# One layer of a hybrid decoder on one core: 12 of 16 n-tiles of the per-layer gate as seven block products

## The chip, the cores and the metric

The kernel runs on one core of a Trainium2 chip. The metric is the device time of one execution in microseconds, from the first instruction to the last; the time before is the median of 3 runs. Engines are named as in the profile: PE (matrix products; PEld its weight loads), DVE (vector), ACT (scalar and table functions), POOL (GpSimd), SP (which only issues DMAs). Each engine works through its own instructions in order; ACT and POOL issue DMAs too.

## What is computed

One layer over 512 prompt tokens and 8 sample tokens, all in float32, D = 2048. Left out here are the norms of queries and keys, the masks and the caches that are handed back:

```python
xn = rmsnorm(x)
q, k, v, gu, gv = split(xn @ w_in)
a = window_attention(q, k, v) @ w_br_attn
m = (gelu(gu) * (W_s @ layernorm(gelu(gv)) + b)) @ w_br_gm          # the gating unit
gB, gA = split(sigmoid(xn @ w_gate + b_gate))
x = x + (gA * a + gB * m) @ w_out
h = causal_conv3(rmsnorm(x) @ w_up)
x = x + (silu(h_gate) * h_up) @ w_down                              # 5632 wide
y = x + sigmoid(rmsnorm(x) @ w_ple_gate) * (p @ w_ple_proj)         # the per-layer gate
```

## The kernel before

**Layout.** Activations lie transposed: a tile holds 128 features by 520 tokens, in two halves of 260 (HW) with 256 prompt and 4 sample tokens each. Tiles of this size live in 67 slots of SBUF (`slot`, NSLOT); some names go to a small extra pool instead (`extra`). A product is taken as three: every float32 operand is split into a rounded part hi and a remainder lo, and hi*hi + hi*lo + lo*hi is summed in PSUM.

**Weights.** They come in blocks of 8 tiles of 128 x 128 (512 KB). `weight_stream` fixes their order for the whole kernel. `block_start(v)` runs as the first tile of block v is used: it issues the loads that are due (SP, three blocks ahead for a plain block), casts block v+2 to hi on ACT, takes its remainder lo on DVE (`cast_block`, `rest_block`), and runs what was put off to this block with `at_block(ahead, f, kind)`, in the order snap, act, dve, end. hi and lo have three buffers each, so ACT casts block v+2 once PE has left block v-1. The order of the instructions is written out by hand; nothing is rescheduled.

**Plain n-tiles.** `ntile` computes one output tile of 128 features from nk input tiles: per weight tile 2 halves x 3 products = 6 matmuls of 260 columns. After each weight tile it advances the generator `self.fine` by one call, so that other work is spread between the tiles.

**Seven block products.** `wpair` computes two n-tiles at once over pairs of k-tiles. Of the 2 x 2 blocks (two n-tiles, two k-tiles, two halves of the tokens) it forms seven products (Strassen's scheme in Winograd's form) in the order P1, P5, P6, P2, P4, P7, P3, each one a block of up to 8 weight tiles with 3 matmuls a tile. The weight sums are made by DVE additions and by POOL DMAs that add while they load (L310, L312). P1, P2 and P3 take halves of the input as they are, the other four take sums of halves; `woperands` builds those and splits them into tiles X. Four PSUM banks collect the outputs; `snap`, `c11`, `c22` and `c12` (L403 to L419) read them.

**Stages.** The front (w_in, attention); `branch_attn` (a = attn @ w_br_attn) with `gmlp`, the gating unit, as its `self.fine`; `gates_plain`, 6 plain n-tiles of w_gate while the operands X are built from x read back from DRAM; `gates_seven`, the other 26 n-tiles; `branch_gm`; `w_out` with p @ w_ple_proj, whose output goes to DRAM (`ppd`); `ffn_up`, all by seven products; `ffn_down`, the k-tiles of w_down in chunks FF_CHUNKS = (6, 14, 6, 12, 6), plain and seven products in turn, where each plain chunk also builds the operands of the next and each chunk but the last adds its output to `x1d` in DRAM; `down_last`, the last chunk, where x stays in SBUF in 16 slots (`self.x1`) and is split into xw; `ple`, the gate by w_ple_gate, 16 plain n-tiles, the last in two halves.

**The gating unit.** `gmlp` is a generator of steps. Each of four chunks of tokens takes two: transposes on PE with statistics on DVE, then the normalisation on DVE (L1298). Each of eight d takes three: the scaling by nw with the split (L1310 to L1312), nothing, then the mix on PE (L1320, L1321) with its sums on DVE. Then come the statistics of the sample tokens (L1332 to L1345), nothing, and their product gx (L1351). `paced` in `branch_attn` leaves 3 weight tiles between two steps.

**Building operands.** `build` takes one operand a call (or `group` of them): `begin` forms the sum on DVE and issues the ACT cast at once, `end` takes the remainder on DVE one call later.

Of the kernel before, what the change touches and what calls it, by code (L numbers as in the profile page):

```python
# [37 lines left out]
PLAIN_GATES = 6  # L38
OUT_GROUP = 3
# [9 lines left out]
FF_CHUNKS = (6, 14, 6, 12, 6)  # L49
# [94 lines left out]
def weight_stream():  # L144
# [26 lines left out]
    for n in range(KD):  # L171
        o.nt("pgate", n, range(KD))
    return o.done()
# [23 lines left out]
class Kernel:  # L197
# [196 lines left out]

    def wpair(self, name, n1, n2, X):

# [24 lines left out]
        after = {"P5": [("snap", lambda: snap("b", "sn", 1))], "P1": [("snap", lambda: snap("a", "sn", 0))], "P2": [("dve", c11)],  # L421
                 "P6": [("snap", lambda: snap("a", "un", 0))], "P7": [("snap", lambda: snap("a", "un", 1)), ("dve", c22)],
                 "P3": [("dve", c12)]}
        for p in PRODUCTS:
# [11 lines left out]
            for kind, f in after.get(p, ()):  # L436
                self.at_block(0, f, kind)
        return c

    def woperands(self, xb):  # L440
# [4 lines left out]
        def begin(p, i):  # L445
# [3 lines left out]
            if p == "P5":  # L449
                src = self.slot(name="tau")[:, 0:HW]  # L450
                nc.vector.tensor_sub(src, b11, b12)
            elif p == "P6":
                nc.vector.tensor_sub(b12, b22, b12)
                nc.vector.scalar_tensor_tensor(out=b11, in0=b12, scalar=-1.0, in1=b11, op0=ALU.mult, op1=ALU.subtract)
                src = b11
            elif p == "P4":
                nc.vector.tensor_add(b21, b21, b11)
                src = b21
            else:
                src = {"P1": b11, "P2": b21, "P7": b12, "P3": b22}[p]  # L460
            x = self.slot(F32R, "X")
            nc.scalar.copy(x[:, 0:HW], src)

            def end():
                nc.vector.tensor_sub(x[:, HW:NT], src, x[:, 0:HW].bitcast(F32))
                X[p][i] = x

            return end
# [95 lines left out]
    def run(self):  # L564
# [62 lines left out]
        with ExitStack() as c2:  # L627
# [11 lines left out]
            self.ffn_down(c3)  # L639
            c3.close()  # L640
            self.slotp = {}
        with ExitStack() as c1:
            self.psum(c1, 2, 4)
            self.down_last()
            self.ple()
# [84 lines left out]
    def branch_attn(self):  # L730
# [48 lines left out]
    def gates_plain(self):  # L779

        nc, a, xn = self.nc, self.a, self.xn
        X = {p: [None] * KQ for p in PRODUCTS}
# [3 lines left out]
        xb = {}  # L786
        self.X, build = self.woperands(xb)
        self.X.update(X)

        def run():  # L790
            for i in range(KQ):
                for k in (2 * i, 2 * i + 1):
                    xb[k] = self.slot(name="xr")
                    nc.sync.dma_start(xb[k][:, 0:NT], a["x"][k])
                yield
                yield
                yield
                yield
                for k in (2 * i, 2 * i + 1):
                    nc.scalar.activation(xb[k][:, 0:NT], xb[k][:, 0:NT], AF.Copy, scale=self.col("an", k))  # L800
# [3 lines left out]
        self.fine = run()  # L804
# [444 lines left out]
    def gmlp(self):  # L1249
# [58 lines left out]
        for d in range(KG):  # L1308
# [3 lines left out]
            h, l = self.split(self.v2(gv[d]), "gn")  # L1312
            yield
            yield
# [16 lines left out]
            yield  # L1331
# [15 lines left out]
        yield  # L1347
# [433 lines left out]
```

## Time and profile before

| | us |
|---|---|
| median of 3 runs (2702.42 to 2703.47) | 2703.02 |
| profiled execution | 2702.04 |
| its span | 2700.3 |

The profiled execution's time is 1.7 us more than its span, from the first to the last instruction of the program. The page gives the busy time of each engine, then the span in 40 slices, the DMA queues, the chain of work that ended last, and the costliest groups. Of the stages, with bounds read from the order of PE's instructions: the front runs to 393 us, w_br_attn and the gating unit to 515, the plain gates to 585, the seven-product gates to 846, w_br_gm to 938, w_out to 1122, p @ w_ple_proj to 1150, the up-projection to 2039, the five chunks of w_down to 2108, 2250, 2319, 2441 and 2511, and the per-layer gate to 2696.

How to read the rows that follow: a row of waits names the waiting group, what it waited for, us in total, times, and the longest. A row of stages gives the stretch, its length, the busy us of PE, PEld, DVE, ACT and POOL (instructions in brackets), the granted clock of PE, the DMA share and GB/s. A row in order of time gives start, us, engine, line, what, count, and in square brackets the idle time before it and what ended it. A row of groups gives the count, busy us, mean ns, and the idle time before.

### The profile page before, as it was taken

What the parts mean: (1) busy time and instruction counts of PE and PEld (TensorE: products, weight loads), DVE (VectorE), ACT (ScalarE), POOL (GpSimd) and SP (SyncE); (2) the same over time, 40 slices, a digit from 0 to 9 for tenths busy, and PEclk for the clock granted to TensorE, in tenths of its full rate; (3) what the DMA queues carried; (4) which work ended last, traced back from release to release, by engine and by line L of the source; (5) the groups of instructions that cost most, each with busy time, mean ns of one, the idle gap of its engine ahead of it and who ended that gap; (6) DMA issues with size and microseconds to landing.
All of it is one profiled execution on the core that took longest, in us unless ns stands there. A gap on an engine that the chain in (4) does not pass through costs nothing.

```text
span 2700.3 us, 53713 instructions
## 1 busy us (share of the span) xinstructions
PE 2673.4 (99%) x22212; PEld 2668.0 (99%) x22212; DVE 1871.6 (69%) x2791; ACT 1287.4 (48%) x2173; POOL 288.4 (11%) x443
## 2 busy tenths in 40 slices
PE   9999999999999999999999999999999999999999
PEld 9999998999999999999999999999999999999999
DVE  6666557567666533688888888888888676576533
ACT  5365452354444233555555555555556445444321
POOL 0111001000010000011111111111111111110000
PEclk9999999999999999999999999999999999999999
DMA  5223323567667444566666666666668677675333
GB/s 188 93 81 102 103 79 122 184 206 204 190 188 239 158 134 142 193 186 171 163 177 174 162 174 174 162 177 171 166 167 249 152 180 204 153 178 183 125 132 106
DMA packets 151797, 438.06 MB, mean 162 GB/s; under 512 B 17200, under 2 KB 18352, under 8 KB 151552
## 3 DMA queue, kind: packets, MB, share of 16 engines
q1 hardware_dynamic: 117504, 337.58, 37.1%
q0 software_dynamic: 29440, 88.53, 18.8%
q10 hardware_dynamic: 4608, 8.52, 0.8%
q8 instruction: 174, 2.85, 0.4%
q14 instruction: 71, 0.58, 0.1%
HBM read 373.23 MB, written 61.33 MB: 161 GB/s over the span
## 4 chain that ended last, share of the span: by engine, by line
PE 96%; DVE 2%; ACT 1%; issue 0%; DMA 0%; POOL 0%; ACTq 0%; SPq 0%; DVEq 0%; POOLq 0%
PE wa L433 22%; PE wb L433 15%; PE mm L372 14%; PE mm L376 14%; PE mm L374 14%; PE wd L433 7%; PE wc L433 7%; PE po L1106 1%; PE s L1043 1%; ACT hi L279 0%; PE pt L1088 0%; PE pl L1654 0%; DVE lo L286 0%; DVE z L1298 0%; ACT z L1256 0%
## 5 line engine op out<-in xcount | busy, mean ns | idle before, releaser
L286 DVE TENSOR_TENSOR lo<-st,hi 128x1024 fp32r<-128x1024 f32 (+3 forms) x352 | 421.9, 1198 | 268.9 <-ACT hi L279 261.3
L433 PE MATMUL wa<-X,hi 128*128 128x260 f32 x3152 | 576.6, 283 | 0.9 <-ACT pp L1427 0.9
L433 PEld LDWEIGHTS wa<-X,hi 128*128 128x128 f32 x3152 | 485.5, 188 | 1.1 <-ACT pp L1427 1.1
L279 ACT CAST hi<-st 128x1024 fp32r<-128x1024 f32 (+3 forms) x352 | 362.3, 1029 | 195.8 <-DMA st<-in_w 83.8
L433 PE MATMUL wa<-X,lo 128*128 128x260 f32 x1576 | 444.7, 282 | 0.0
L433 PE MATMUL wb<-X,hi 128*128 128x260 f32 x2032 | 371.5, 283 | 0.0
L279 ACT CAST hi<-S 128x1024 fp32r<-128x1024 f32 (+2 forms) x219 | 222.6, 1017 | 230.0 <-DVE S L312 171.7
L286 DVE TENSOR_TENSOR lo<-S,hi 128x1024 fp32r<-128x1024 f32 (+2 forms) x219 | 258.5, 1180 | 99.9 <-ACT hi L279 99.6
L433 PEld LDWEIGHTS wb<-X,hi 128*128 128x128 f32 x2032 | 312.8, 188 | 0.0
L433 PEld LDWEIGHTS wa<-X,lo 128*128 128x128 f32 x1576 | 296.7, 188 | 0.0
L433 PE MATMUL wb<-X,lo 128*128 128x260 f32 x1016 | 286.7, 282 | 0.0
L286 DVE TENSOR_TENSOR lo<-L,hi 128x1024 fp32r<-128x1024 f32 (+2 forms) x146 | 172.5, 1181 | 125.0 <-ACT hi L279 124.6
L372 PE MATMUL mm<-xn,hi 128*128 128x260 f32 x1088 | 222.9, 286 | 5.3 <-ACT hi L279 5.3
L376 PE MATMUL mm<-xn,lo 128*128 128x260 f32 x1088 | 219.6, 283 | 0.0
L374 PE MATMUL mm<-xn,hi 128*128 128x260 f32 x1088 | 219.3, 283 | 0.0
L279 ACT CAST hi<-L 128x1024 fp32r<-128x1024 f32 (+2 forms) x146 | 148.4, 1016 | 121.3 <-PE wd L433 118.8
L433 PE MATMUL wd<-X,hi 128*128 128x260 f32 x1120 | 205.1, 283 | 0.0
L310 POOL DMA_DIRECT2D L<-in_w x73 | 63.3, 867 | 1265.5 <-issue 828.9
L433 PEld LDWEIGHTS wb<-X,lo 128*128 128x128 f32 x1016 | 191.4, 188 | 0.0
L372 PEld LDWEIGHTS mm<-xn,hi 128*128 128x128 f32 x1088 | 168.4, 190 | 5.4 <-ACT hi L279 5.3
L433 PEld LDWEIGHTS wd<-X,hi 128*128 128x128 f32 x1120 | 172.2, 188 | 0.1
L376 PEld LDWEIGHTS mm<-xn,lo 128*128 128x128 f32 x1088 | 168.8, 189 | 0.0
(313 smaller groups left out, 5966.8 us busy)
## 6 DMA issues: line engine op xcount, KB each, us to landing
st<-in_w SPq DMA_DIRECT2D x317, 512.0 KB, 4.4
S<-in_w SPq DMA_DIRECT2D x57, 512.0 KB, 3.5
S<-in_w POOLq DMA_DIRECT2D x57, 512.0 KB, 7.9
L<-in_w SPq DMA_DIRECT2D x57, 512.0 KB, 4.0
L<-in_w POOLq DMA_DIRECT2D x57, 512.0 KB, 5.6
fd<-hb SPq DMA_DIRECT2D x44, 260.0 KB, 2.2
fr<-fd SPq DMA_DIRECT2D x44, 260.0 KB, 4.9
xr<-in_x SPq DMA_DIRECT2D x32, 260.0 KB, 4.2
```

The lines of the kernel that those rows point to most:

```text
L279: self.nc.scalar.copy(self.hi[v][:, c], self.st[WS.src[v]][:, c])
L286: self.nc.vector.tensor_sub(self.lo[v][:, c], self.st[WS.src[v]][:, c], self.hi[v][:, c].bitcast(F32))
L310: self.nc.gpsimd.dma_start(self.st[kind, r][:, c], self.a["w"][src][:, c], accum_op=ALU.add)
L372: mm(ps[:, h, 0:HW], lhsT=whi, rhs=xh[h], start=start, stop=False)
L374: mm(ps[:, h, 0:HW], lhsT=whi, rhs=xl[h], start=False, stop=False)
L376: mm(ps[:, h, 0:HW], lhsT=wlo, rhs=xh[h], start=False, stop=stop)
L433: nc.tensor.matmul(ps(z), lhsT=w, rhs=x, start=new and i == 0 and q == 0, stop=i == len(X[p]) - 1 and q == 2, skip_group_check=True)
L1043: nc.tensor.matmul(out, lhsT=self.cols(q, c), rhs=keys(kk, c), start=n == 0, stop=n == 1)
L1106: nc.tensor.matmul(po[:, kb * 128:kb * 128 + w], lhsT=vv[:, kb * 128:(kb + 1) * 128], rhs=pp[:, o:o + w], start=kb == 0 and n == 0, stop=k ...
```

## The change

1. The per-layer gate: `ple` becomes `ple_plain`, 4 plain n-tiles (PLAIN_PLE), and `ple_seven`, 12 n-tiles in 6 pairs. Before, x1 stayed in SBUF; now `down_last` also writes it to `x1d` and splits it into two halves a tile, `ple_plain` reads it back to build the operands (`sum_operands`, which is `gates_plain`'s builder made general), and each output tile reads p @ w_ple_proj and x1 again (`y_load`). The last pair finishes by hooks in `wpair`.
2. The gating unit: steps 4 weight tiles apart; the split for d+1 is issued a step ahead of the mix of d, and the sample statistics ahead of all mixes.
3. Operands in three steps: sum, cast, remainder, each one call later than the one before.
4. FF_CHUNKS = (5, 14, 5, 14, 6), and the builder there takes two calls for every fourth step only, in place of every second.
5. `c21`, the last part of the second output, is formed as P3 begins, not after it.

```diff
+PLAIN_PLE = 4
-FF_CHUNKS = (6, 14, 6, 12, 6)
+FF_CHUNKS = (5, 14, 5, 14, 6)
...
-    for n in range(KD):
+    for n in range(PLAIN_PLE):
         o.nt("pgate", n, range(KD))
+    for n in range(PLAIN_PLE, KD, 2):
+        o.winograd("pgate", n, n + 1, range(KD))
...
+        def c21():
+            nc.vector.tensor_sub(part("c2", 0), ps("d"), part("un", 1))
+
         def c12():
             nc.vector.tensor_add(part("c1", 1), ps("b"), part("un", 0))
-            nc.vector.tensor_sub(part("c2", 0), ps("d"), part("un", 1))
...
         def build(items, every=1, group=1):
-            ends = []
-            while items or ends:
+            hi, lo = [], []
+            while items or hi or lo:
                 for _ in range(every if isinstance(every, int) else next(every)):
                     yield
-                now, items = items[:group], items[group:]
-                new = [begin(*x) for x in now]
-                for e in ends:
-                    e()
-                ends = new
+                for f in lo:
+                    f()
+                for f, _ in hi:
+                    f()
+                lo = [f for _, f in hi]
+                new = [steps(*x) for x in items[:group]]
+                items = items[group:]
+                for f, _, _ in new:
+                    f()
+                hi = [f[1:] for f in new]
...
         def paced():
             for _ in g3:
-                yield
-                yield
-                yield
+                yield from [None] * 4
...
+    def sum_operands(self, xn, src, w):
...
         def run():
             for i in range(KQ):
                 for k in (2 * i, 2 * i + 1):
                     xb[k] = self.slot(name="xr")
-                    nc.sync.dma_start(xb[k][:, 0:NT], a["x"][k])
...
+                    nc.sync.dma_start(xb[k][:, 0:NT], src[k])
+                yield from [None] * 3
                 for k in (2 * i, 2 * i + 1):
-                    nc.scalar.activation(xb[k][:, 0:NT], xb[k][:, 0:NT], AF.Copy, scale=self.col("an", k))
+                    nc.scalar.activation(xb[k][:, 0:NT], xb[k][:, 0:NT], AF.Copy, scale=self.col(w, k))
                 yield from build([(p, i) for p in ("P5", "P6", "P4", "P7")], 1)
...
+        hl = parts(0)
+        yield
         g = [self.slot(name="gn") for _ in range(2)]
         ag, rs = stats(banks, NS)
...
         yield
-        yield
+        for d in range(KG):
+            new = parts(d + 1) if d + 1 < KG else None
+            yield
+            mix(d, *hl)
+            hl = new
+            yield
         p = self.aux("gx")
...
-                    X, self.fine = self.down_operands(ch[c + 1], cycle((1, 2)))
+                    X, self.fine = self.down_operands(ch[c + 1], cycle((1, 1, 1, 2)))
...
+        def parts(n):
+            self.xw[n] = self.split_halves(x1[n], "yw", self.col("pn", n))
+            t = x1.pop(n)
+            self.at_block(1, lambda: nc.sync.dma_start(self.x1d[n], t[:, 0:NT]))
...
+    def ple_plain(self):
+        nc = self.nc
+        self.X, self.fine = self.sum_operands(self.xw, self.x1d, "pn")
+        yl = self.y_load(0)
+        for n in range(PLAIN_PLE):
+            p = self.ntile("pgate", n, range(KD), self.xw)
+            self.drain(self.gr)
+            t = self.slot(name="pg")
+            nc.vector.tensor_mul(self.v2(t), self.pv(p), self.v2(self.R))
+            fs = self.y_end(n, lambda t=t: t, yl)
+            self.at_block(0, fs[1], "act")
+            self.at_block(1, fs[2], "dve")
+            self.at_block(1, fs[3])
+            if n + 1 < PLAIN_PLE:
+                yl = self.y_load(n + 1)
+        self.finish_fine()
+        self.xw = None
+
+    def ple_seven(self):
+        h0, h1 = slice(0, HW), slice(HW, NT)
+        for n in range(PLAIN_PLE, KD - 2, 2):
+            c = self.wpair("pgate", n, n + 1, self.X)
+            for i in range(2):
+                self.y_blocks(i + 1, self.y_end(n + i, lambda c=c, i=i: c[f"c{i + 1}"], self.y_load(n + i)))
...
+        def first(c):
+            y.extend((self.y_load(n), self.y_load(n + 1)))
+            self.y_blocks(0, self.y_end(n, lambda: c["c1"], y[0], h0))
+
+        def second(c):
+            for f in self.y_end(n + 1, lambda: c["c2"], y[1]):
+                self.at_block(0, f)
+
+        c = self.wpair("pgate", n, n + 1, self.X, {"P4": first, "P7": second})
+        self.flush()
+        for f in self.y_end(n, lambda: c["c1"], y[0], h1):
+            f()
```

`y_load` issues two loads on SP (p @ w_ple_proj and x1 of tile n) into the extra pool's four buffers; `y_end` returns four steps for an output tile: times R on DVE, sigmoid on ACT, times p and plus x1 on DVE, the store on SP; `y_blocks` puts them off by up to two blocks.

More of the change, by code (lines that the diff above doesn't have):

```diff
@@ L443, in woperands, with steps, own, hi @@
         X = {}
-        def begin(p, i):
+        def steps(p, i):
             k1, k2 = xb[2 * i], xb[2 * i + 1]
             b11, b12, b21, b22 = k1[:, 0:HW], k1[:, HW:NT], k2[:, 0:HW], k2[:, HW:NT]
[L449 to L464, printed above, removed]
+            src = {"P1": b11, "P2": b21, "P6": b11, "P4": b21, "P7": b12, "P3": b22}.get(p)
+            x = None
+            def own():
+                nonlocal src
+                if p == "P5":
+                    src = self.slot(name="tau")[:, 0:HW]
+                    nc.vector.tensor_sub(src, b11, b12)
+                elif p == "P6":
+                    nc.vector.tensor_sub(b12, b22, b12)
+                    nc.vector.scalar_tensor_tensor(out=b11, in0=b12, scalar=-1.0, in1=b11, op0=ALU.mult, op1=ALU.subtract)
+                elif p == "P4":
+                    nc.vector.tensor_add(b21, b21, b11)
+            def hi():
+                nonlocal x
+                x = self.slot(F32R, "X")
+                nc.scalar.copy(x[:, 0:HW], src)
+            def lo():
@@ L1306, in bc, with parts @@
             return z.rearrange("p (h c w) -> p h c w", h=1, c=1).to_broadcast([128, 2, 2, 128])
-        for d in range(KG):
+        def parts(d):
             w = nw[d // 4][:, (d % 4) * 128:(d % 4) * 128 + 128]
@@ L1311, in gmlp, with mix @@
             nc.gpsimd.dma_start(a["gp_o"][:, d * 128:(d + 1) * 128], self.cols(gv[d], 3))
[L1312 to L1314 removed]
+            return self.split(self.v2(gv[d]), "gn")
+        def mix(d, h, l):
             ps = [self.aux("mx") for _ in range(2)]
@@ L1614, in down_last @@
             del self.f[j]
-        self.finish_fine()
-        xw[KD - 1] = self.split(self.v2(self.x1[KD - 1]), "yw", scale=self.col("pn", KD - 1))
-        self.xw = xw
+        parts(KD - 1)
         self.R = self.slot(name="R3")
@@ L1620, in down_last, with y_load @@
         self.bg.append(self.gr)
-    def ple(self):
-        nc, a = self.nc, self.a
-        pp = {}
-        def load(n):
-            if n < KD:
-                pp[n] = self.slot(name="pp")
-                nc.sync.dma_start(pp[n][:, 0:NT], self.ppd[n])
-        load(0)
-        load(1)
-        for n in range(KD - 1):
-            load(n + 2)
+    def y_load(self, n):
+        t = [self.slot(name="yl") for _ in range(2)]
+        self.nc.sync.dma_start(t[0][:, 0:NT], self.ppd[n])
+        self.nc.sync.dma_start(t[1][:, 0:NT], self.x1d[n])
+        return t
@@ new lines, in y_end, with times_r, sigmoid, rest @@
+    def y_end(self, n, t, yl, c=slice(0, NT)):
+        nc = self.nc
+        pp, x1 = yl
+        def times_r():
+            nc.vector.tensor_mul(t()[:, c], t()[:, c], self.R[:, c])
+        def sigmoid():
+            nc.scalar.activation(t()[:, c], t()[:, c], AF.Sigmoid)
+        def rest():
+            nc.vector.tensor_mul(t()[:, c], t()[:, c], pp[:, c])
+            nc.vector.tensor_add(t()[:, c], t()[:, c], x1[:, c])
+        def store():
+            nc.sync.dma_start(self.a["y_o"][n][:, c], t()[:, c])
+        return times_r, sigmoid, rest, store
@@ L1636, in ple, with y_blocks @@
+    def y_blocks(self, b, fs):
+        for i, (f, kind) in enumerate(zip(fs, ("dve", "act", "dve", "end"))):
+            self.at_block(b + min(i, 2), f, kind)
+    def ple_plain(self):
+        nc = self.nc
+        self.X, self.fine = self.sum_operands(self.xw, self.x1d, "pn")
+        yl = self.y_load(0)
+        for n in range(PLAIN_PLE):
             p = self.ntile("pgate", n, range(KD), self.xw)
             self.drain(self.gr)
-            g = self.slot(name="pg")
-            nc.vector.tensor_mul(self.v2(g), self.pv(p), self.v2(self.R))
```

74 lines of the change are left out of this document (27 added, 47 removed).

## The prediction

> **What bounds the kernel now.** I read the page first, its busy times and the chain that ended last.
>
> ```profile
> span 2700.3 us, 53713 instructions
> PE 2673.4 (99%) x22212; PEld 2668.0 (99%) x22212; DVE 1871.6 (69%) x2791; ACT 1287.4 (48%) x2173; POOL 288.4 (11%) x443
> PE 96%; DVE 2%; ACT 1%; issue 0%; DMA 0%; POOL 0%; ACTq 0%; SPq 0%; DVEq 0%; POOLq 0%
> ```
>
> TensorE (PE) is busy all but 26.9 us of the span and holds 96% of the chain. So time changes in two ways only: by the number of matmuls, or by the stalls and slow clock of PE. The chain in order of time gives the price of a matmul, and the list of waits, for PE alone, gives the stalls.
>
> ```profile
> 585.08 2.88 PE wa L433 x24
> ```
>
> ```profile
> PE mm L372 <- ACT hi L279: 5.3, 1, 5.3
> PE mx L1320 <- ACT gnh L490: 3.7, 1, 3.7
> PE mm L372 <- ACT pp L1427: 2.6, 3, 1.4
> PE gx L1351 <- DVE dgs L1344: 2.2, 1, 2.2
> PE g L1294 <- DVE z L1298: 2.0, 3, 0.8
> ...
> PE mx L1321 <- DVE gnl L491: 0.6, 2, 0.4
> ```
>
> A block of 24 matmuls of 260 columns takes 2.88 us, 0.120 us each; a plain weight tile (6 matmuls) takes 0.72 us and a block of eight of them 5.77 us. Of the stalls, the rows mx, gx, g and mx, 8.5 us, are all of the gating unit, which runs in steps beside the product of w_br_attn. The table of stages shows that two of them cost more than the wait, since the granted clock (PEclk) falls afterwards:
>
> ```profile
> 425.00:429.10 4.10, 0.38 (x5) 0.18 (x3) 3.27 (x10) 0.69 (x2) 0.53 (x2) 1.00 0.43 128
> 429.10:433.20 4.10, 3.75 (x17) 3.55 (x18) 2.83 (x5) 1.48 (x2) 0.20 (x1) 0.60 0.22 81
> ...
> 491.70:494.30 2.60, 0.36 (x4) 0.18 (x2) 2.53 (x7) 0.96 (x1) 0.60 (x2) 1.00 0.30 109
> 494.30:501.60 7.30, 7.30 (x36) 7.28 (x37) 2.50 (x11) 0.00 (x0) 0.48 (x1) 0.53 0.62 223
> ```
>
> At 0.60 of the clock 4.1 us lose 1.6 us, and at 0.53 7.3 us lose 3.4 us: 5.0 us on top of 8.5, so the unit costs 13.5 us.
>
> **Part 1, the matmuls.** Four weight tiles cost 4 x 6 = 24 matmuls plainly and 7 x 3 = 21 by seven products, for 2 n-tiles and 2 k-tiles. The gate: 12 n-tiles x 16 k-tiles x 6 = 1152 become 6 pairs x 8 x 21 = 1008, so 144 fewer. The chunks of w_down: 26 of 44 k-tiles by seven products become 28; a k-tile is 16 x 6 = 96 matmuls plainly and 84 otherwise, so 2 x 12 = 24 fewer. Together 168 fewer, 168 x 0.120 = **-20.2 us**, all on the bounding engine.
>
> **Part 2, the gating unit.** Its steps stand 4 weight tiles apart, not 3, and the operands of one mix are split one d earlier. The normalisation first; VectorE (DVE) in order of time, the first and last of four:
>
> ```profile
> 407.29 2.64 DVE L1298 TENSOR_SCALAR z<-g,sm,sm 128x128 f32<-128x128 f32 x8 [0.70 <-POOL sm L1287]
> ...
> 425.14 2.64 DVE L1298 TENSOR_SCALAR z<-g,sm,sm 128x128 f32<-128x128 f32 x8 [0.44 <-POOL sm L1287]
> ```
>
> (425.14 - 407.29)/3 = 5.95 us of DVE per chunk. PE now gives it two steps, 6 x 0.72 = 4.3 us and some 0.8 us of transposes, so it stalls; then it will give 8 x 0.72 + 0.8 = 6.6 us. The wait of 2.0 goes, but with only 0.6 us to spare a chunk. The first mix now follows its split by 6 tiles (4.3 us); then three steps lie between, 12 tiles or 8.6 us, against a wait of 3.7, so it goes with its clock loss. The product gx is issued one step behind its statistics and waits 2.2 us; then all eight mixes lie between. Bounds: nothing, if DVE stays as late as PE moves, and 13.5. I take **-12.5**, 1.0 short of all for the thin margin.
>
> [...]
>
> **Part 3, the gate's new stages.** For a pair of n-tiles DVE will do 7 weight remainders, 2 weight sums, 4 output parts and 2 x 3 passes over an output. The first and the last row come from the old gate stage, the others from the existing seven-product stage:
>
> ```profile
> L286 DVE TENSOR_TENSOR lo<-st,hi 128x1024 fp32r<-128x1024 f32 x28 | 34.2, 1222 | 73.0 <-ACT hi L279 73.0
> ...
> L1641 DVE TENSOR_TENSOR pg<-pg,pp 128x520 f32<-128x520 f32 x14 | 9.8, 700 | 9.9 <-ACT pg L1640 9.9
> ```
>
> ```profile
> L312 DVE TENSOR_TENSOR S<-S,st 128x1024 f32<-128x1024 f32 x5 | 6.1, 1225 | 0.2
> ...
> L410 DVE TENSOR_TENSOR c<-wc,sn 128x260 f32<-128x260 f32 x6 | 2.5, 422 | 0.3 <-PE wc L433 0.3
> ```
>
> 7 x 1.22 + 2 x 1.23 + 4 x 0.42 + 6 x 0.70 = 16.9 us against 7 x 2.88 = 20.2 us of PE: 84%, hidden. The up-projection shows that more is hidden too; its row and the existing seven-product gate's:
>
> ```profile
> 1149.00:2036.00 887.00, 885.27 (x7372) 884.77 (x7373) 764.02 (x1014) 482.33 (x797) 140.82 (x264) 1.00 0.65 171
> ```
>
> ```profile
> 590.00:690.00 100.00, 100.00 (x837) 100.00 (x837) 71.48 (x82) 47.29 (x63) 8.76 (x10) 1.00 0.74 206
> ```
>
> DVE is 86% busy there and PE loses 1.7 us in 887. Cost 0.
>
> The seam between the plain and the seven-product tiles isn't hidden. Operands are built in 9 calls for each of 8 pairs of k-tiles, 72 in all, but 4 plain n-tiles make only 64. The eighth pair's loads go out with the last tile, and its whole build then stands in ScalarE's (ACT's) queue ahead of the weight cast for the third block, P6. The trace has the same build where there is room for it:
>
> ```profile
> 564.13 1.35 ACT L800 ACTIVATE xr<-xr,cvt 128x520 f32<-128x520 f32 x2
> ...
> 567.74 0.41 ACT L462 CAST X<-xr 128x260 fp32r<-128x260 f32 x1 [0.28 <-DVE xr L457]
> 571.25 0.41 ACT L462 CAST X<-xr 128x260 fp32r<-128x260 f32 x1 [3.11 <-DMA gd<-gv]
> 571.57 1.04 ACT L279 CAST hi<-st 128x1024 fp32r<-128x1024 f32 x1
> ```
>
> ```profile
> xr<-in_x SPq DMA_DIRECT2D x32, 260.0 KB, 4.2
> ```
>
> From the first scaling to the third cast 4.0 us pass, with the fourth 4.4 (without its wait for a free slot); cast and remainder of the weights add 1.0 + 1.2, so 6.6 us from landing. P6 starts two blocks, 5.8 us, after the plain tiles end. If the loads have landed by then PE stalls 0.8 us; if they are only issued then, 4.2 later, 5.0. A build wholly ahead of PE costs 0. Engines run ahead of PE wherever no slot or buffer holds them; I take **+2.0**, and keep 0 and 5.0, with 1.6 more for the clock (the row of 0.60).
>
> **Part 4, the larger chunks.** The first plain chunk has 5 tiles a column, 16 x 5 = 80 calls, and its builder needs 79 (7 pairs x 9 steps, each fourth step two calls). P3, built last, is needed 6 blocks later, so this hides. DMA is nearer its limit:
>
> ```profile
> DMA packets 6533, 16.15 MB, mean 234 GB/s; under 512 B 736, under 2 KB 736, under 8 KB 6526
> ```
>
> ```profile
> 2070.00:2080.00 10.00, 10.00 (x85) 10.00 (x84) 8.38 (x21) 6.53 (x15) 2.60 (x3) 1.00 1.00 226
> ```
>
> ```profile
> 2050.00:2090.00 40.00, 40.00 (x336) 40.00 (x335) 31.33 (x66) 25.01 (x55) 9.10 (x11) 1.00 0.99 254
> ```
>
> The stage's 16.15 MB less two weight blocks (1.05) are 15.1 MB in 80 x 0.72 = 57.7 us. At the 254 GB/s of its full stretch that takes 59.4 us, at the 226 of the slowest 66.8: 1.7 or 9.1 us over. The next chunk needs less, and weights are loaded three blocks (17 us) ahead, so I take **+0.5** and keep 0 and 9.1. [...]
>
> **Part 5, three-step operands and the end.** Casts wait less for DVE, which matters only beside p @ w_ple_proj, where PE waits 2.6 for ACT; there the copies to DRAM hold ACT too. Bounds -2.6 and +1; I take 0. The end, in order of time, now:
>
> ```profile
> 2695.86 0.43 DVE L1656 TENSOR_TENSOR pg<-pl,R 128x260 f32<-128x260 f32 x1 [3.92 <-PE pl L1654]
> 2696.33 0.42 ACT L1657 ACTIVATE pg<-pg 128x260 f32<-128x260 f32 x1 [5.31 <-DVE pg L1656]
> 2696.78 0.43 DVE L1658 TENSOR_TENSOR pg<-pg,pp 128x260 f32<-128x260 f32 x1 [0.49 <-ACT pg L1657]
> 2697.24 0.43 DVE L1659 TENSOR_TENSOR pg<-pg,x 128x260 f32<-128x260 f32 x1
> ```
>
> Behind P3 comes one more addition (0.43). In P3's 2.88 us DVE and ACT must also do two parts (0.85), three passes over the other n-tile (3 x 0.70) and its sigmoid (0.64): with the handovers about 3.9, so the last half starts some 0.8 late. **+1.2**, bounds 0.4 and 2.
>
> **Sum.** -20.2 - 12.5 + 2.0 + 0.5 + 1.2 = -29.0. The profiled execution took 2702.0 us, 1.7 more than its span; it becomes 2673.0. The median of the runs is 1.0 above it, so I forecast **2674.0 us**.
>
> ```profile
> DMA packets 151797, 438.06 MB, mean 162 GB/s; under 512 B 17200, under 2 KB 18352, under 8 KB 151552
> ...
> S<-in_w SPq DMA_DIRECT2D x57, 512.0 KB, 3.5
> ```
>
> **The rivals.** (a) The seam or the full DMA queue stalls PE: 5.0 - 2.0 + 1.6 for the seam and up to 8.6 for the chunk, 2679 to 2687. For it: the 64 calls against 72, the share of 1.00; against it: the lookahead. (b) The gating unit's stalls stay: 12.5 more, 2686.5; half of them, 2680. That is the change not doing what it says. For it: 0.6 us of margin; against it: 12 tiles between split and mix. A milder form: the clock falls to 0.53 for another reason than the stall of gx, and 3.4 us stay, 2677.4; the two rows that stand next to each other speak against it, so it has 0.05 of the forecast's chance, and it lies in its range. [...] (c) All gains come in and the seam and pproj cost nothing or gain: 2674 - 1.0 - 2.0 - 2.6 = 2668. (d) Slower: the seven-product gate starves for DMA. A pair moves 6 x 0.524 MB of weights (512 KB each, the row above) and 6 x 0.266 of inputs and outputs (260 KB each), 4.74 MB in 20.2 us, 235 GB/s. If only the mean rate of the whole run, 162, came through, a pair would take 29.3 us, 6 x 9.1 = 55 us more, 2729. It decides below 6 x 4.74 / (121 + 29) = 190 GB/s. Against it: 206 GB/s pass at a share of 0.74, and 254 at 0.99.
>
> **How the numbers follow.** Forecast, 2669 to 2679: 0.62; (a) 0.18; (b) 0.11; (c) 0.06; (d) 0.03. The range 2667 to 2685 takes in (c), most of (a) and the milder half of (b). A measurement tells about 0.2%, 5.4 us, from no change: every case but (d) is faster by more, so 0.96 faster, 0.01 the same, 0.03 slower.
>
> **What would show it.** The page should count 22044 matmuls. Between 393 us and the end of w_br_attn's product the waits for gnh, dgs and z should be gone and PEclk 1.00. The gate should run in two parts, 384 matmuls and 1008; in the second's first three blocks, P6's wait for ACT or DVE tells the seam's price. The first plain chunk should take 57.7 us with no wait for hi or lo. The prediction is wrong if PE waits for DMA or weights in the seven-product gate, or if the plain chunks stall.

## The result and the profile after

| | before | after |
|---|---|---|
| median of 4 runs, us | 2702.97 (2702.42 to 2703.47) | 2681.76 (2680.13 to 2682.74) |
| ratio to before | | 0.9921, 95% interval 0.9904 to 0.9938 |
| profiled execution, its span | 2702.04, 2700.3 | 2681.24, 2679.5 |
| the forecast | | 2674.0 (2667 to 2685) |

The kernel became 21.2 us faster, where 29.0 were forecast. The time lies in the range, but 7.8 us of the gain are missing, and it lies above the 2669 to 2679 that had 0.62 of the chances. The stages, with bounds read from the order of PE's instructions as in the first part, show where they went:

| stage, us | before | after | difference | forecast |
|---|---|---|---|---|
| front | 388.13 | 388.37 | +0.2 | 0 |
| w_br_attn and gating unit | 121.72 | 109.95 | -11.8 | -12.5 |
| plain and seven-product gates | 331.13 | 331.05 | -0.1 | 0 |
| w_br_gm, w_out, p @ w_ple_proj, up-projection | 1192.60 | 1192.09 | -0.5 | 0 |
| first four chunks of w_down | 402.33 | 397.71 | -4.6 | -2.9 + 0.5 |
| last chunk | 69.29 | 69.23 | -0.1 | 0 |
| per-layer gate | 185.31 | 178.80 | -6.5 | -17.3 + 2.0 |
| last matmul to end of span | 4.51 | 7.16 | +2.6 | +1.2 |

The shortfall is in the row of the per-layer gate, 6.5 in place of 15.3, and in a smaller way at the end; the chunks of w_down gave back 2.2 more than forecast. The busy times on the page of after come first:

```profile
span 2679.5 us, 53765 instructions
PE 2654.1 (99%) x22044; PEld 2648.1 (99%) x22044; DVE 1948.0 (73%) x2930; ACT 1337.8 (50%) x2280; POOL 295.5 (11%) x455
```

The 168 matmuls are gone to the last one (22212 to 22044), and PE is still the engine that sets the time. Its idle time fell only from 26.9 to 25.4 us: the stalls of the gating unit went and others came. The list of PE's waits of after (what waited, for what, us in total, times, the longest) shows which:

```profile
PE mm L375 <- ACT hi L282: 5.2, 1, 5.2
PE wb L438 <- ACT X L473: 2.5, 1, 2.5
PE wa L438 <- ACT sn L409: 2.1, 1, 2.1
PE mm L375 <- ACT pp L1452: 1.9, 4, 0.6
...
PE wb L438 <- DVE lo L289: 0.9, 1, 0.9
PE wb L438 <- DVE X L476: 0.8, 2, 0.5
```

No row for gnh, dgs or z is left. The rows wb and wa are new: they are the second and third blocks, P5 and P6, of the first pair of seven-product tiles in the last gate. The table of stages of after places them (stretch, length, busy us of PE, PEld, DVE, ACT, POOL, granted clock, DMA share, GB/s). The rows are the gating unit, the first plain chunk of w_down, the two stretches behind the plain tiles of the last gate, and the rest of that gate:

```profile
393.00:502.00 109.00, 107.76 (x883) 106.42 (x882) 74.09 (x158) 39.34 (x57) 13.68 (x24) 0.98 0.44 148
2026.70:2084.30 57.60, 57.60 (x481) 57.60 (x480) 47.25 (x98) 35.57 (x79) 12.20 (x16) 1.00 0.89 250
2543.00:2553.50 10.50, 5.05 (x29) 3.79 (x27) 9.37 (x20) 6.02 (x14) 1.75 (x2) 0.84 0.89 215
2553.50:2561.00 7.50, 6.61 (x32) 6.61 (x33) 6.03 (x6) 3.98 (x8) 0.00 (x0) 0.54 0.44 128
2561.00:2670.00 109.00, 109.00 (x912) 109.00 (x911) 83.91 (x100) 49.47 (x69) 7.78 (x9) 1.00 0.72 209
```

The first two rows and the last are close to the forecast: a clock of 0.98 (1.00 was expected) and hardly a stall in the gating unit, not one in the plain chunk although DMA moves 250 GB/s there, none in the seven-product gate behind its first blocks. The third and fourth rows hold the loss: PE stands half of 10.5 us and then runs at 0.54 of its clock. The pair's first 21 x 8 = 168 matmuls should take 168 x 0.120 = 20.2 us; worked out matmul by matmul, 11.0 us are lost between 2543.3 and 2561. That is the seam of the prediction, five times as dear as the +2.0 in its sum.

**Why the seam is dear.** ACT's instructions in order of time, from the first scaling of a pair of operands (L812) to the last, with what stands behind that:

```profile
2496.82 1.34 ACT L812 ACTIVATE xr<-xr,cvt 128x520 f32<-128x520 f32 x2
...
2501.65 1.28 ACT L537 ACT_TABLE_LOAD   x1
2506.91 0.64 ACT L537 ACTIVATE ry<-ry 128x520 f32<-128x520 f32 x1 [3.99 <-DVE ry L535]
2507.46 0.39 ACT L473 CAST X<-xr 128x260 fp32r<-128x260 f32 x1
2507.76 1.35 ACT L812 ACTIVATE xr<-xr,cvt 128x520 f32<-128x520 f32 x2
...
2548.56 1.34 ACT L812 ACTIVATE xr<-xr,cvt 128x520 f32<-128x520 f32 x2
...
2552.50 1.04 ACT L282 CAST hi<-S 128x1024 fp32r<-128x1024 f32 x1
2553.45 0.63 ACT L1665 ACTIVATE pg<-pg 128x520 f32<-128x520 f32 x1
2553.98 0.35 ACT L409 COPY sn<-wa 128x260 f32<-128x260 f32 x1
```

The builder gives a pair 9 calls, one a weight tile, 9 x 0.722 = 6.5 us. The first scaling stands 3 us behind the start of the stage (2493.59). The second comes 10.94 us after it, 4.4 too late, because ACT stood 3.99 us at the square root (L537) of the last norm, waiting for DVE. The six behind it come at (2548.56 - 2507.76)/6 = 6.8 us each: the 4.4 us are never worked off, they grow to 6.2. What DVE did meanwhile is the norm's chain that makes R, again in order of time:

```profile
2502.80 0.76 DVE L531 TENSOR_SCALAR rv<-ss 128x260 f32<-128x260 f32 x2
2503.48 1.77 DVE L533 RECIPROCAL ry<-rv 128x260 f32<-128x260 f32 x1
2505.16 1.72 DVE L535 RECIPROCAL ry<-rv 128x260 f32<-128x260 f32 x1
2507.59 0.70 DVE L539 TENSOR_TENSOR rt<-ry 128x520 f32<-128x520 f32 x1 [0.70 <-ACT ry L537]
...
2509.52 0.70 DVE L542 TENSOR_TENSOR R<-ry,rt 128x520 f32<-128x520 f32 x1
```

From 2502.80 to 2510.2 DVE does nothing else, 7.4 us, and the builder needs DVE, ACT and DVE again for each operand. So the last pair is scaled at 2548.56, 8.1 us after the plain tiles end (2540.47), and PE waits for it twice:

```profile
2550.58 0.59 PE L438 MATMUL wb<-X,hi 128*128 128x260 f32 x1 [2.52 <-ACT X L473]
2551.48 0.58 PE L438 MATMUL wb<-X,hi 128*128 128x260 f32 x1 [0.31 <-DVE X L476]
2554.39 0.80 PE L438 MATMUL wa<-X,hi 128*128 128x260 f32 x2 [2.11 <-ACT sn L409]
```

First P5, the second block, waits for its own operands (X); then P6 waits for the copy of P1's result out of its bank (sn, L409), which stands in ACT's queue behind the last build and a weight cast (the rows 2552.50 to 2553.98 above).

### The profile page after: what moved, and what is told of

It is laid out like the page before. It is cut to its first block, busy times and chain, and to the rows that moved or that the text cites. A ratio compares the mean times of both kernels' runs of the same rounds, so it can differ in the third digit from the quotient of the medians.

```text
span 2679.5 us, 53765 instructions
## 1 busy us (share of the span) xinstructions
PE 2654.1 (99%) x22044; PEld 2648.1 (99%) x22044; DVE 1948.0 (73%) x2930; ACT 1337.8 (50%) x2280; POOL 295.5 (11%) x455
## 3 DMA queue, kind: packets, MB, share of 16 engines
q0 software_dynamic: 31168, 95.35, 20.2%
## 5 line engine op out<-in xcount | busy, mean ns | idle before, releaser
L438 PE MATMUL wa<-X,hi 128*128 128x260 f32 x3392 | 621.0, 283 | 3.0 <-ACT sn L409 2.1
L289 DVE TENSOR_TENSOR lo<-st,hi 128x1024 fp32r<-128x1024 f32 (+2 forms) x336 | 404.4, 1204 | 183.4 <-ACT hi L282 179.5
L438 PEld LDWEIGHTS wa<-X,hi 128*128 128x128 f32 x3392 | 523.2, 189 | 3.5 <-ACT sn L409 2.4
L438 PE MATMUL wa<-X,lo 128*128 128x260 f32 x1696 | 478.3, 282 | 0.0
L282 ACT CAST hi<-st 128x1024 fp32r<-128x1024 f32 (+2 forms) x336 | 347.8, 1035 | 114.5 <-PE mm L377 50.5
L282 ACT CAST hi<-S 128x1024 fp32r<-128x1024 f32 (+1 forms) x237 | 244.3, 1031 | 251.6 <-DVE S L315 181.5
L289 DVE TENSOR_TENSOR lo<-S,hi 128x1024 fp32r<-128x1024 f32 (+1 forms) x237 | 283.7, 1197 | 96.2 <-ACT hi L282 94.8
L289 DVE TENSOR_TENSOR lo<-L,hi 128x1024 fp32r<-128x1024 f32 (+1 forms) x158 | 189.3, 1198 | 134.4 <-ACT hi L282 129.5
L282 ACT CAST hi<-L 128x1024 fp32r<-128x1024 f32 (+1 forms) x158 | 162.7, 1030 | 130.8 <-PE wd L438 129.0
L438 PE MATMUL wd<-X,lo 128*128 128x260 f32 x616 | 173.5, 282 | 0.0
```

The lines of the kernel that those rows point to most:

```text
L282: self.nc.scalar.copy(self.hi[v][:, c], self.st[WS.src[v]][:, c])
L289: self.nc.vector.tensor_sub(self.lo[v][:, c], self.st[WS.src[v]][:, c], self.hi[v][:, c].bitcast(F32))
L438: nc.tensor.matmul(ps(z), lhsT=w, rhs=x, start=new and i == 0 and q == 0, stop=i == len(X[p]) - 1 and q == 2, skip_group_check=True)
```

## The experiments

All are variants of the changed kernel; each ratio is to the kernel before, in runs of the same chip, with its 95% interval.

**1. Six plain n-tiles.** If the stall is one of a late builder, two more n-tiles give it 32 more calls, at the price of 24 matmuls.

```diff
-PLAIN_PLE = 4
+PLAIN_PLE = 6
```

> Six plain n-tiles of the gate in place of four (PLAIN_PLE = 6), the rest as changed. Theory T: the operand builder is late at the seam because the norm's chain for R holds DVE and ACT for some 7 us at its start and nothing leaves room to catch up; 32 more calls (23 us) give that room, so the seam's 10.9 us (6.3 us of waits, the rest clock) go and 24 more matmuls cost 2.9: about 2673.5. Rival C, too few calls (64 of 72), says the same. Rival S, the stores on SP that hold the loads behind them, leaves part of the seam: 2676 to 2680. If none of them holds, 2684.5 (the matmuls alone).

Measured 2674.49 us (2673.41 to 2675.07), ratio 0.989 (0.9875 to 0.9905). The gate takes 69.90 + 100.88 = 170.78 us, 8.0 less than with four plain tiles: 2.9 more for matmuls and 10.9 less at the seam. The seam is worth 11 us and nothing else in the gate is late. T and C expected the same here, so this run does not tell them apart.

**2. The builder starts three n-tiles earlier.** It is made as the last chunk's n-tile 13 begins, and takes each tile of xw as it comes up.

```diff
         for n in range(KD):
             load(n + 2)
+            if n == 13:
+                self.X, self.fine = self.sum_operands(self.xw, self.x1d, "pn")
```

> Four plain n-tiles, but the builder of the operands starts at the 14th n-tile of the last chunk of w_down, 18 calls earlier, so it has 82 calls for its 72. T: the lag of 6 us left by the norm's chain fits into the 10 spare calls (7.2 us), so the seam costs at most 1: about 2671.5. C: about 2671. S: part of the seam stays, 2673 to 2679. If the slots (67) hold the builder instead, 2676 or more.

Measured 2678.55 us (2676.99 to 2679.78), ratio 0.9905 (0.989 to 0.992). The gate falls to 48.37 + 125.43 = 173.80: 4.4 us of the seam are left, and the plain part takes 1.5 more than after. So T and C, about 2671, fell. The time lies where S and the slots had it; S falls with run 4, and this run's list of waits shows no long wait of ACT or DVE for a free slot. The last pair is now scaled 1.0 us before the plain tiles end (2542.54 against 2543.55), and in the first blocks behind them PE waits 2.8 us for remainders and a cast of the weights, and no longer for X. Calls alone, even ten to spare, did not empty the queues.

**3. The norm's chain left out.** R stays the mean square; reciprocals, square root and refinement are not done.

```diff
-        self.gr = self.norm_chain(self.acc, self.R)
+        self.gr = short(self.acc, self.R)
         self.bg.append(self.gr)
```

> As changed, but the chain that makes R of the last norm is cut to its first two DVE instructions (0.8 us): the reciprocals, the square root and the Newton step, some 6.5 us in DVE's queue with a wait of 4 us in ACT's, are left out, so y differs. T: the builder runs some 6 us sooner, and of the seam's 10.9 us about 2 stay: 2673. C and S: the number of calls and the order on SP are the same, so it stays at 2680 to 2682.

Measured 2674.62 us (2673.04 to 2675.65), ratio 0.989 (0.9876 to 0.9905). The gate's second part falls from 131.91 to 123.61, with 2.9 us of the seam left. The chain carries 8 of the 11 us.

**4. SP's order.** In the trace of after a store of y waits 16.5 us on SP, with the next pair's loads behind it. Here the plain tiles' stores go out from POOL.

```diff
-            self.at_block(1, fs[3])
+            self.at_block(1, lambda n=n, t=t: nc.gpsimd.dma_start(self.a["y_o"][n], t[:, 0:NT]))
```

> As changed, but the four stores of y in the plain part are issued by POOL and not by SP, so no load of operands stands behind a store that waits for DVE. S: the loads go out up to 9 us sooner and the seam shrinks by 4 us or more: 2677 or less. T and C: DVE and ACT are late for other reasons, within 1.5 us of 2681.5.

Measured 2680.0 us (2678.95 to 2681.59), ratio 0.9909 (0.9893 to 0.9926); the seam costs 10.80. The order of SP is not the cause: in after ACT waits only 1.3 us in all for these loads, and the engines that use them are later still.

**5. Both: early builder and no chain.** After runs 2 and 3 two causes stood side by side.

> The builder of the last gate starts three n-tiles earlier, and the reciprocals, square root and refinement of the last norm are left out (y is then scaled by another factor). Alone, the first left 4.4 us of the stall and the second 2.95 us of 11.0. Theory (two causes that add: the norm's chain of 7.4 us on DVE with its 4 us wait on ACT, and the 8 calls that are missing): nothing is left, the gate's two parts take 46.1 + 121.0 us, and the time is about 2674.6 - 2.95 = 2671.7 or up to 1 less. Rival (the passes over y and the weight remainders on DVE hold the builder whatever its start): 2 to 3 us stay, 2674.

Measured 2670.19 us (2669.89 to 2671.34), ratio 0.9877 (0.9863 to 0.989). The table of stages of this run shows the plain part and the first blocks behind it:

```profile
2493.40:2540.20 46.80, 46.80 (x389) 46.68 (x388) 38.96 (x81) 31.27 (x58) 0.00 (x0) 1.00 0.60 204
2540.20:2561.00 20.80, 20.80 (x176) 20.80 (x175) 15.31 (x17) 8.96 (x12) 1.75 (x2) 1.00 0.86 255
```

PE is busy all the time at full clock; the two parts take 46.88 + 120.88 us (46.1 + 121.0 were expected). Either cause alone leaves a part (4.4 and the 1.5 of the plain part with the chain, 2.9 with the late start), both gone leave nothing. The two overlap and do not add: taken away alone they give 8.1 and 5.1 us, more than 11.0 together. The 2.9 are what the prediction had argued, 72 calls into 64; the chain was missing from it.

**6. Operands in two steps again.** The builder is that of the kernel before: sum and cast in one call, the remainder in the next, so a pair takes 8 calls and eight pairs fit the 64 exactly. So this run takes away a call as well as a step: in the kernel before a pair had 9 in the plain gates, with four calls, not three, between its loads and its scaling.

```diff
-                for f in lo:
-                    f()
-                for f, _ in hi:
-                    f()
...
+                now, items = items[:group], items[group:]
+                new = [begin(*x) for x in now]
+                for e in ends:
+                    e()
+                ends = new
```

> Operands built in two steps again (sum with cast, remainder), all else as changed. A pair then takes 8 calls, so 8 pairs fit exactly into the 64 calls of the 4 plain n-tiles. If the 72 calls against 64 were the whole cause of the stall behind the plain tiles of the last gate, it goes, from 11.0 us to 0 to 1: time about 2671 to 2672. If the lag that the norm's chain leaves is the cause, as the run without the chain says, the last pair's scaling comes at most 7 calls, 5.1 us, earlier and some 6 us or more of the stall stay: 2676.5 or more. On the waits of PE for DVE c L418 that the kernel before had at the change from seven products to plain (4.4 us in three): if the three steps took them away they come back (about 4 us more in the chunks of w_down), if the moved c21 did they stay gone.

Measured 2694.65 us (2694.64 to 2696.62), ratio 0.9968 (0.9955 to 0.998): 12.9 us slower than the change. ACT's scalings of the first and the last pair in this run, and PE's largest waits:

```profile
2504.65 1.35 ACT L803 ACTIVATE xr<-xr,cvt 128x520 f32<-128x520 f32 x2
...
2562.78 1.50 ACT L803 ACTIVATE xr<-xr,cvt 128x520 f32<-128x520 f32 x2 [3.76 <-DMA xr<-x1d]
```

```profile
PE mm L375 <- ACT hi L282: 6.5, 3, 5.1
PE mm L375 <- ACT dn L1597: 3.3, 2, 1.7
PE mm L375 <- ACT pp L1443: 2.9, 3, 1.5
PE wa L438 <- ACT sn L409: 2.4, 1, 2.4
```

A pair takes (2562.78 - 2504.65)/7 = 8.3 us here, although only 8 calls, 5.8 us, are asked for. So the count of calls alone does not set the builder's pace. In the plain chunks of w_down the trace points to the turns between DVE and ACT: with two steps each ACT cast is issued right behind the sum that it needs, and ACT stands in its queue until DVE gets there, 16.6 us in the first plain chunk against 11.1 in after. In the last gate it is another thing, since ACT waits less for DVE there (9.2 us against 16.2) and more for the loads of x1. What it waits for them in this run, and then in after:

```profile
ACT xr L803 <- DMA xr<-x1d: 13.4, 5, 3.9
```

```profile
ACT xr L812 <- DMA xr<-x1d: 1.3, 2, 0.7
```

The loads stand on SP behind stores of y, which wait for DVE: one store goes out at 2529.61, the loads behind it at 2530.04, and the scaling that needs them at 2532.91, 3.9 us after ACT was free for it. Run 4 tried SP's order with three steps only, so how much of the 12.9 us this order takes stays open.

The gate's two parts take 51.75 + 132.32, 5.3 us more than after; the two plain chunks of w_down 60.35 and 59.75 in place of 57.70 and 57.86, 4.5 more, where PE now waits for ACT's copies (dn), though the second takes up to 58.75 in other runs; the plain gates, which have the same builder, 71.15 in place of 69.75. These 1.4 us are not the two steps' own: the kernel before had two steps there as well, in 9 calls a pair, and 69.75 us. The front (+1.9) and w_br_attn (-1.5), which build no operands, differ between the two profiled executions by themselves. The expectation that the count was enough fell. The other one, 2676.5 or more, holds, but the last pair's scaling does not come earlier: it stands 9.6 us behind the plain tiles' end, 8.1 in after. The waits for c L418 did not come back (the list of before has 1.5 us in two of them, not the 4.4 in three of the expectation).

**7. The gating unit, a square of order and distance.** Old order 3 tiles apart, new order 3 apart, old order 4 apart; the change itself is the fourth corner. The edit for the distance, and for the order the old loop:

```diff
-                yield from [None] * 4
+                yield from [None] * 3
...
-        for d in range(KG):
-            new = parts(d + 1) if d + 1 < KG else None
-            yield
-            mix(d, *hl)
...
+        for d in range(KG):
+            h, l = self.split(self.v2(gv[d]), "gn")
+            yield
+            yield
```

Old order, 3 apart:

> All of the change but its second part: the gating unit has its old order and a distance of 3 tiles. By the stage of the two profiles (121.7 against 110.0 us) 11.8 us more: 2693.5; by the prediction's term 12.5 more, 2694. If the waits there were hidden anyway, 2681.5.

New order, 3 apart:

> The gating unit in its new order, but 3 tiles apart as before. If the order alone removes the waits of the mixes and of gx, with their clock loss (3.7 + 0.6 + 2.2 + 5.0 = 11.5 us), only the waits for the normalised z come back: 2 to 3 us more than the changed kernel, 2684. If the distance does it, most of 11.8 comes back: 2690 or more.

Old order, 4 apart:

> The gating unit's steps in the old order, but 4 weight tiles apart; all else as changed. With the runs of both (109.95 us for the stage), of neither (121.7) and of the new order alone (118.4) it completes the square. Theory A (the two parts add up): the distance alone gains 8.5, stage 113.2, time 2681.8 + 3.3 = 2685.0. Theory B (the distance does it all, the order only seems to help where the steps are near): stage 110, time 2681.8. Theory C (each needs the other, since between split and mix 8 tiles, 5.8 us, stand against the 4.3 + 3.7 = 8.0 us that the mix needed before, and gx stays one step behind its statistics): waits for gnh of about 2.2 us and for dgs of about 1.5 us stay, with clock loss, stage 114 to 118, time 2686 to 2690.

| | stage, us | median, us | ratio to before |
|---|---|---|---|
| old order, 3 apart | 121.69 | 2695.8 (2694.19 to 2696.82) | 0.9973 (0.9963 to 0.9984) |
| new order, 3 apart | 118.41 | 2691.99 (2691.52 to 2693.66) | 0.996 (0.9945 to 0.9975) |
| old order, 4 apart | 115.53 | 2691.91 (2691.15 to 2693.41) | 0.9958 (0.9944 to 0.9971) |
| new order, 4 apart (the change) | 109.95 | 2681.76 | 0.9921 (0.9904 to 0.9938) |

The old order at 3 tiles is 14.0 us slower than the change by the medians and 11.7 by the stage; the other 2.3 lie outside that stage. The new order at 3 comes out where its expectation had the distance as the cause (2690 or more). The waits of PE in the new order at 3 tiles, then all that the unit waits for in the old order at 4:

```profile
PE mx L1337 <- ACT gnh L506: 2.8, 1, 2.8
...
PE g L1311 <- DVE z L1315: 2.0, 3, 0.8
...
PE mx L1338 <- DVE gnl L507: 0.9, 3, 0.4
```

```profile
PE gx L1368 <- DVE dgs L1361: 6.7, 1, 6.7
```

The table of stages of the second, behind that wait:

```profile
505.50:515.50 10.00, 10.00 (x48) 9.97 (x49) 2.52 (x11) 0.00 (x0) 0.49 (x1) 0.53 0.56 207
```

So each part takes away other waits. The distance removes those for the normalisation and for the mixes. The order alone leaves those for the normalisation and moves that of the mixes: the first mix, which waited 3.7 us before, starts without a wait at 429.10, and the second waits 2.8 us, until 438.07, since the statistics of the sample tokens now stand ahead of its scaling on DVE:

```profile
429.70 1.28 DVE L1298 BATCH_NORM_STATS2 sm<-g 8x6 f32<-8x512 f32 x2
...
435.01 0.61 DVE L1364 TENSOR_SCALAR dgs<-ident,cvt 8x8 f32<-8x8 f32 x4
...
436.68 0.67 DVE L1327 TENSOR_TENSOR z<-z,nw 128x512 f32<-128x512 f32 x1
```

The order removes the wait of gx, and at the wider distance it is needed more than before: the old order has three steps for each d, and 4 tiles apart they no longer fit the 128 tiles of the stage. The last mix, the statistics and gx come behind the last tile in one go, so gx waits 6.7 us, and 2.8 us of clock are lost in the plain gates that follow (72.51 against 69.75). Theories A (113.2) and B (110) fell. 115.5 falls into the interval of C (114 to 118), but only half by its reason: the wait for gnh was gone, and the one for dgs was 6.7 us, not 1.5. The time, 2691.9, is above C's 2690, by the clock lost in the plain gates.

**8. The old gate, and the old chunks.** With all else as changed: `ple` of before; FF_CHUNKS and the builder's cycle of before.

```diff
-FF_CHUNKS = (5, 14, 5, 14, 6)
+FF_CHUNKS = (6, 14, 6, 12, 6)
...
-                    X, self.fine = self.down_operands(ch[c + 1], cycle((1, 1, 1, 2)))
+                    X, self.fine = self.down_operands(ch[c + 1], cycle((1, 2)))
```

The old gate:

> All of the change but its first part: the per-layer gate is the old one, 16 plain n-tiles with x kept in SBUF. By the stages of the two profiles the gate gained 6.5 us and the end lost 2.65, so this takes 3.9 us more than the changed kernel: about 2685.5. By the sum of the prediction (17.3 for the matmuls less 2.0 and 1.2) it would be 14.1 more, 2695.5.

The old chunks:

> The chunks of w_down as before, (6, 14, 6, 12, 6), with two calls for every second step of the builder. 24 more matmuls are 2.9 us more: 2684.5. By the stages of the two profiles it was 4.6 us: 2686. If the fuller DMA queue cost the larger chunks something, the difference is below 2.9.

The old gate gave 2686.56 us (2683.98 to 2692.44), ratio 0.9936 (0.9919 to 0.9953), its stage 185.29: the gate's part of the change is worth 6.5 us by the stage, and 4.8 by the medians, since the end is shorter there (4.82 against 7.16); the 14.1 us of the prediction's sum fell. The four runs spread over 8.5 us, and the profiled one is the slowest: 4.5 us of that stand in the plain gates (74.23 against 69.75), which the edit leaves alone. The old chunks gave 2685.83 us (2683.03 to 2686.67), ratio 0.9935 (0.992 to 0.9949), and 400.3 us for the four chunks: 2.6 of the change's 4.6 us are the matmuls (2.9 by the count). The other 2 are for the most part a wait that only the trace of before shows, in its list of waits:

```profile
PE mm L372 <- DVE c L418: 1.5, 2, 0.9
```

There the first plain tile behind a stage of seven products waits while DVE reads the last two banks in `c12`. In after it starts (2225.31) before c12 does (2225.51), so it does not need the bank that c12 still reads; the other one, d, is read by c21, since the change at the start of P3. The wait is gone with the old chunks and with the two-step builder too, and what these share with the change is the moved c21. That makes it the likely cause, though the row names c12, which stands ahead of c21 in before; it was not undone alone.

**9. Six plain n-tiles and a new end.** The first half of the last but one n-tile is finished beside P7, the last n-tile goes in two halves, and the second of its rests is put behind the scaling of the last half.

```diff
-            self.y_blocks(0, self.y_end(n, lambda: c["c1"], y[0], h0))
+            r, sg, rest, store = end(c, n, "c1", y[0], h0)
+            self.at_block(0, r, "dve")
+            for f in (sg, rest, store):
+                self.at_block(0, f)
...
+            a, b = end(c, n + 1, "c2", y[1], h1), end(c, n + 1, "c2", y[1], h0)
+            for f in (a[0], a[1], b[0], b[1], a[2], a[3]):
                 self.at_block(0, f)
...
-        for f in self.y_end(n, lambda: c["c1"], y[0], h1):
-            f()
+        b, e = y[2], end(c, n, "c1", y[0], h1)
+        e[0]()
+        e[1]()
+        b[2]()
+        b[3]()
+        e[2]()
+        e[3]()
```

> Six plain n-tiles in place of four, as in the earlier run with six (2674.5 us), and a new order on DVE behind the last matmuls: the first half of the last but one n-tile is finished beside P7, the last n-tile is taken in two halves, and its second rest stands behind the scaling of the last half, beside the sigmoid. Theory (the end is late because passes that could run earlier stand ahead of c12 on DVE): c12 starts within 0.2 us of its matmul, then 0.42 + 0.46 + 0.9 + 0.9 = 2.7 us on DVE and 2.9 us for the store, so the end falls from 7.16 us to about 5.7; the time is 2674.5 - 1.4 = 2673.1. Rival (the end is set by ACT or by the landing of the stores, not by DVE's order): the end stays at 7 us or above and the time at 2674.5. This is also the fastest version that the earlier runs point to.

Measured 2672.89 us (2671.09 to 2673.65), ratio 0.9885 (0.9871 to 0.9898): the fastest of the kernels that leave nothing of the layer out, 8.9 us ahead of the change. DVE at the end of after, where the last matmul ends at 2672.38, and of this run, where it ends at 2665.78:

```profile
2672.90 0.70 DVE L1669 TENSOR_TENSOR c<-c,yl 128x520 f32<-128x520 f32 x1
2673.52 0.42 DVE L1668 TENSOR_TENSOR c<-c,yl 128x260 f32<-128x260 f32 x1
2673.97 0.43 DVE L1669 TENSOR_TENSOR c<-c,yl 128x260 f32<-128x260 f32 x1
2674.32 0.42 DVE L424 TENSOR_TENSOR c<-wb,un 128x260 f32<-128x260 f32 x1
...
2676.16 0.43 DVE L1669 TENSOR_TENSOR c<-c,yl 128x260 f32<-128x260 f32 x1
```

```profile
2665.82 0.43 DVE L424 TENSOR_TENSOR c<-wb,un 128x260 f32<-128x260 f32 x1
...
2667.89 0.43 DVE L1669 TENSOR_TENSOR c<-c,yl 128x260 f32<-128x260 f32 x1
```

c12 (L424) starts at once in place of 1.9 us late, the last pass ends 2.5 us after the last matmul in place of 4.2, and the span 2.9 us behind that in both. The end takes 5.40 in place of 7.16 us.

## Why the prediction was right, and where it was not

- **Matmuls, -20.2: right.** The count is met exactly, and where nothing else happens the stage shows it: with six plain tiles the gate is at 69.90 + 100.88 us without a loss.
- **The gating unit, -12.5: right, 11.8 measured.** The waits of 8.5 us and most of the low clock behind them went. A stretch at 0.51 of the clock is left, 488.5 to 492.0 us, and makes the 0.98. The reasons hold for z, which the distance takes away, and for gx, which the order does. For the mixes the prediction counted the tiles between split and mix, and either part alone is enough for the first mix; that the new order puts the sample statistics ahead of the second, so that it needs the distance too, it did not see. The rival that the stalls stay falls.
- **DVE at 84% in the gate's new stages, 0: right.** From 2561 us on PE has no loss, at 83.91 us of DVE in 109.
- **The seam, +2.0: the step that failed.** The mechanism was named and its place found, but the term was mis-sized: 11.0 us. It was priced as one build, the last pair's, before P6's weight cast, on the ground that "Engines run ahead of PE wherever no slot or buffer holds them". That part was sound by itself: without the norm's chain 2.9 us are left. What was overlooked is that the chain for R, 7.4 us of DVE and a wait of 4 us on ACT, now falls among the first calls of the builder. Before, it stood beside plain tiles that asked little of either engine (from 2510.52 to 2560 DVE was busy 26.5 of 49.5 us and ACT 15.9, and PE all the time). Runs 3 and 5 show it: 8 of the 11 us go with the chain, all with the chain and the late start. The upper bound of 5.0 + 1.6 was too low for the same reason; rival (a), 2679 to 2687 with 0.18, is what happened, in its half about the seam. That the time still lies in rival (a)'s interval is partly luck: the seam passed its bound by 4.4 us, and the chunks, with 2.2 us more gain than forecast, and the DMA queue, which cost nothing, made up for it.
- **Larger chunks, +0.5: right.** The plain chunk took 57.70 us, 80 x 0.72, without a wait, at 250 GB/s and a DMA share of 0.89; so the bound of 9.1 fell, and the half of rival (a) that rested on the full DMA queue. The rival of a starving gate fell as well: 209 GB/s at a share of 0.72 there, and no wait for weights.
- **Operands in three steps, 0: mis-sized.** The prediction saw a use beside p @ w_ple_proj alone (that stage gained 0.6). In this kernel three steps in 9 calls a pair are worth 12.9 us by the medians against two steps in 8, 11 of them in the last gate, the chunks of w_down and the plain gates (5.3 + 4.5 + 1.4): they carry the larger chunks, which the sum took for hidden by itself. How much is due to the steps and how much to the call and to SP's order was not taken apart. Their value does not show as a gain against before, where the smaller chunks with two steps took 69.23 and 69.20 us, as much as with three (69.02 and 69.22 in the run with the old chunks).
- **The moved c21: left out of the sum.** It was costed only at the end, and the waits for c L418, 1.5 us in two, were in the list of before. They are most of the 2 us that the chunks gained beyond their matmuls, with the moved c21 as the likely cause, not a shown one.
- **The end, +1.2: mis-sized, +2.6.** The prediction's list of what falls beside P3 left out the rest of the first half (the 128x260 rows of L1668 and L1669, 0.8 us). It stands with the rest of the other n-tile ahead of c12 on DVE, so c12 starts 1.9 us after its matmul, not 0.8. Run 9 shows that the order does it.
- **The clock behind the stalls, 5.0 us of the unit's 13.5: two thirds right.** The prediction's rows have 1.6 us of low clock behind the wait of 3.7 us and 3.4 behind the one of gx, 2.24 us. In after both waits are gone and the clock is 1.00 from 393 to 488 us, so the 1.6 went. But behind the 16 small matmuls of gx (L1376, 486.37 to 488.3 us), which now start without a wait, the clock is still 0.51 from 488.5 to 492.0, 1.7 us lost: that part came without the stall, as the milder form of rival (b) had it for all of the 3.4. 8.5 + 5.0 - 1.7 = 11.8 is what the stage gained. In the seam the two longest gaps are 2.5 and 2.1 us, and the granted clock is 0.50 from 2550.19 us on, within the first of them.

The sum by what was measured: -20.2 - 11.8 + 11.0 - 1.7 + 2.6, and -0.5 for the small differences of the other stages, makes -20.6, against the 20.8 between the two spans.

## What to carry to other kernels

When a generator of background work is put into a stage, list everything else that now falls into the same calls, one-off chains such as a norm's reciprocals above all: here a delay of 4.4 us at the second pair was not worked off, since a pair took 6.8 us where 6.5 were asked for; it was 6.2 us at the last pair, and it was paid in one piece where the first consumer stands, 11.0 us with the clock. Count the pace by the turns between the engines (sum, cast, remainder) and by the loads that each pair needs, not by the number of calls alone: three turns in 9 calls were 12.9 us better here than two in 8. Where a dear seam can be had away with some more of the slower work (here 24 matmuls, 2.9 us, for 11 us), try the size of the split before anything else.

## What the hardware showed

The price of a stall in clock did not follow its length: the prediction's rows lose 1.6 us behind a stall of 3.7 and 3.4 us behind one of 2.24; behind gaps of 2.5 and 2.1 us in the seam, with few matmuls between, the granted clock was 0.54 for 7.5 us, and behind the 6.7 us of gx 0.53 for 10 us, which is 4.7 us lost; behind gx in after, without a stall, it was 0.51 for 3.5 us. The seam's 11.0 us are 6.3 us of gaps (0.9, 0.5, 2.5, 0.3 and 2.1) and 4.7 us of clock. DMA took 250 GB/s in the plain chunk at a share of 0.89 without one wait of PE, and in the same chunk of before PE was busy for all of the 40 us at a share of 0.99 and 254 GB/s (the prediction's row), so a share near 1 in the profile alone was no sign that the stage is bound by it.
